# A kernel's build-time scheduler gets other durations for the instructions of each engine, and another delay between engines

## The chip, the cores and the metric

The kernel runs on one core of a Trainium2 chip. The metric is the device time of one execution, in microseconds (us), lower is better; a kernel's figure is the median of its runs. Engines are named as the profile names them: PE (TensorE), DVE (VectorE), ACT (ScalarE), POOL (GpSimd) and SP (SyncE, which issues DMA transfers).

## The reference, cut to what matters

One decoder block over 2048 positions with 1024 channels, in float32:

```
u    = rms_norm(x, norm1_gain);  proj = u @ w_in            # 1024 -> 3072
x_lru, g_lru, q, k, v, g_ret = split(proj)                  # six parts of 512
xc   = causal_conv4(x_lru);  hl = rg_lru(xc, gates)         # scan over positions
y_lru = rms_norm(hl * gelu(g_lru))
o    = head_group_norm(retention(rotary(q), rotary(k), v))  # 4 heads, chunks of 128
h    = x + concat(y_lru, o * silu(g_ret)) @ w_out           # 1024 -> 1024
u    = rms_norm(h, norm2_gain)
up   = causal_conv3(u @ ffn_up_w);  a, b = split(up)        # 1024 -> 6144
h    = h + (gelu(a) * b) @ ffn_down_w                       # 3072 -> 1024
return rms_norm(h, final_norm_gain)
```

## The kernel before, in words

**The matmuls.** A float32 product is made of three passes in a reduced float32 format: a high part times a high part, and each low part times the other's high part. The tiles are named for that: `wh` and `wl` (or `wv`) are the parts of the weights, `bh` and `raw` (`bl`) those of the activations. The high part is cut by ACT (`wh<-s`, `bh<-raw`), the low part by DVE (`wl<-s,wh`, `raw<-raw,bh`). Large matrix products are cut into units, and a unit into seven products instead of eight: sums of quadrants of the weights (`s`) and of the activations (named 11, T1, T2, 21, T3, T4, 22) are multiplied and combined again. One product is twelve matmuls of 128x512. The first four units (tile `pq`) and the output projection use the plain eight products. The banks in PSUM have the tags `x`, `y`, `e` and `sm` (1, 2, 2 and 3 of them): `px`, `py` and `pe` are the products of a unit, and `py` goes on accumulating after one partial result has been read out of it (that reading is called `u2` in the code).

**The stages.** Input projection (0 to about 320 us of the profile, its heads up to about 550), output projection (up to about 640), up-projection (640 to 1690), down projection (1690 to the end). Each is done in two halves of 1024 positions. Between the products of the projections stand small float32 matmuls: transposes of `o` (`pt<-idt,o`), the retention (`sc`, `pk`, `po`), the gates of the recurrence (`pa`, `pg`), sums for the norms (`mst`). A norm's factor goes one way through several engines: DVE (`ms`) to POOL (power of -0.5) to PE (transpose `pt<-idt,ms`) to ACT (`rb`) to SP (a row to memory and back, spread over the partitions).

**What sets the order.** The program is written as many generators (processes), one for each piece of work, each of which yields its operations in turn. A list scheduler (class `Flow`) runs them when the kernel is built, with a clock for each engine. In `run`, of all engines that one is taken whose next operation could start first; of its operations that are ready by then, the one of lowest rank (its priority, which comes from the tick at which it is due) is issued, and recorded as the next instruction of that engine. So the planned times decide one thing alone: the order of the instructions on each engine. On the chip each engine takes its instructions strictly in that order and waits for semaphores.

Four things enter the planned times. `Engine.cost_pe`, `cost_v`, `cost_a` and `cost_p` (from L129 on) give an operation's duration. `ready` gives the time at which its inputs are written and its output is free, and adds 0.2 us if the other engine is not the same. `issue` advances the engine's clock, adds 1.28 us when ACT has to load another table, and 0.1 us to the end of every operation of PE. The SP clock is held to the planned end of the transfers less `BACKLOG`. Slots of SBUF and banks of PSUM are handed out at planned times too (`grant`, `free`).

All instructions of the compute engines are recorded by one helper, so in the profile all of them stand on L127; DMA issues stand on L365 and, for the norms' rows, L1014.

Of the kernel before, what the change touches and what calls it, by code (L numbers as in the profile page):

```python
# [26 lines left out]
F32R = mybir.dt.float32r  # L27
AF = mybir.ActivationFunctionType
# [17 lines left out]
SMALL = 150  # L46
ORDER = ("l0 q0 v0 l1 q1 v1 l2 q2 v2 q3 v3 l3", "l3 q0 v0 l0 q1 v1 q2 v2 l1 q3 v3 l2")
RATE = 330.0
LATE = 16
PLAIN = 4  # L50
SOON = 2.5
# [26 lines left out]
ANY_TABLE = (AF.Copy, AF.Identity, AF.Square)  # L78
# [27 lines left out]
class Engine:  # L106
# [23 lines left out]

    def cost_pe(self, op, n, args, kw):
        if op == "transpose":
            return 0.13
        one = max(0.03, 0.0133 + n / 2400)
        if args[1].shape[0] == 64:
            one /= 2
        return one if args[1].dtype == F32R else 4 * one

    def cost_v(self, op, n, args, kw):
        if op == "tensor_tensor_scan":  # L140
            return 0.2 + 2.1e-3 * n
        if op in ("tensor_scalar", "tensor_copy", "memset"):
            return 0.15 + 0.535e-3 * n
        if op == "reciprocal":
            return 0.15 + 6.1e-3 * n
        if op == "bn_stats":
            return 0.3
        if op == "scalar_tensor_tensor":
            return 0.2 + 1.06e-3 * n
        return 0.15 + 1.05e-3 * n  # L150

    def cost_a(self, op, n, args, kw):
        us = 0.17 + 0.86e-3 * n
        if isinstance(kw.get("scale"), bass.AP):
            us += 0.1
        if isinstance(kw.get("bias"), bass.AP):
            us += 0.09
        if "accum_out" in kw:
            us += 0.2
        return us  # L160

    def cost_p(self, op, n, args, kw):
        return 0.1 if op == "dma_start" else max(1.0, 0.3 + 2.2e-3 * n)


class Event:
# [31 lines left out]
class Flow:  # L198
# [33 lines left out]
    def ready(self, op):  # L232
        t = 0.0
        for name in op.reads:
            w = self.wrote.get(name)
            if w:
                t = max(t, w[0] + (0.0 if w[1] == op.eng else 0.2))
        for name in op.writes:
            for table in (self.wrote, self.read):
                w = table.get(name)  # L240
                if w:
                    t = max(t, w[0] + (0.0 if w[1] == op.eng else 0.2))
        return t

    def issue(self, op, start):
        us = op.us
        if op.eng == "a" and op.func is not None and op.func not in ANY_TABLE and op.func not in self.table:
            self.table = next(t for t in TABLES if op.func in t)
            us += 1.28
        end = start + us  # L250
        self.clock[op.eng] = end
        if op.kb:
            end = self.dma = max(start + 1.7, self.dma) + op.kb / RATE
        if op.eng == "pe":
            end += 0.1
        for c in op.calls:
            c()
        for name in op.reads:
            if self.read.get(name, (0,))[0] < end:
                self.read[name] = (end, "dma" if op.kb else op.eng)  # L260
        for name in op.writes:
            self.wrote[name] = (end, "dma" if op.kb else op.eng)
# [65 lines left out]
def hymba_block_kernel(ctx: ExitStack, tc: tile.TileContext, xh, xn, win, wout, wup, down, gates, vecs,  # L328
# [1227 lines left out]
    def stage_b(g):  # L1556
        st = RawStage("B", g, m_d[g])
        ng = NormGroup(V_N2, u_d[g].put, h_d[g][0], LATE * g)
        us = []
# [160 lines left out]
```

## Time and profile before

| | |
|---|---|
| time, median of 3 runs | 2167.18 us |
| lowest, highest | 2165.2, 2167.5 us |
| span of the profiled execution | 2165.3 us (the execution's own time lies among the three above) |
| PE busy | 2143.6 us (99%), 9848 matmuls |
| DVE busy | 1729.8 us (80%), 2185 instructions |
| ACT busy | 1226.1 us (57%) |
| POOL busy | 38.3 us (2%) |
| DMA | 404.69 MB, 187 GB/s in the mean |

How to read it: a row of the timeline has its start and its duration in us, engine, line, operation, output and inputs, sizes, and how many are merged; in brackets stands the idle time before it and whom it waited for. A matmul's modelled duration (0.39 us) overlaps its neighbours', so a busy PE is not a measure of its speed; the distance from start to start is. In the view of waits, a row says who waited for whom: us in total, how many times, the longest.

### The profile page before, as it was taken

To read this page: it belongs to the slowest core of one execution; us is meant where nothing else is said; L and a number is where in the kernel's file an instruction comes from. 1 tells how busy PE (TensorE), PEld (TensorE's weight loads), DVE (VectorE), ACT (ScalarE), POOL (GpSimd) and SP (SyncE) were. 2 spreads that over 40 slices of the span, in tenths; PEclk is the share of its full clock that TensorE was granted. 3 is DMA by queue.
4 is the path that set the end of the run, shared out by engine and by line. 5 is a ranking of instruction groups with operands and counts; after the bars stand their busy time and mean duration, and the time that the engine had idled before them with its cause. 6 is when DMAs were issued, how large, how long until landed. Compare 5 with 4: busy or idle time off the path is not lost.

```text
span 2165.3 us, 26460 instructions
## 1 busy us (share of the span) xinstructions
PE 2143.6 (99%) x9848; PEld 1768.5 (82%) x9848; DVE 1729.8 (80%) x2185; ACT 1226.1 (57%) x1768; POOL 38.3 (2%) x32
## 2 busy tenths in 40 slices
PE   9999999999999999999999999999999999999998
PEld 7878887888878888888888888888888888888887
DVE  6999896877854789988878988787878977777776
ACT  6774668555652266666666866666666544334432
POOL 0000000000000000000000000000000000000000
PEclk9999999999999999999999999999999999999999
DMA  8966444431657935544233432322335777667674
GB/s 327 377 210 226 141 163 118 160 111 58 226 185 275 390 132 180 185 141 156 98 106 128 175 127 98 122 98 100 105 107 185 260 299 261 232 255 278 237 258 189
DMA packets 140768, 404.69 MB, mean 187 GB/s; under 512 B 15920, under 2 KB 20448, under 8 KB 140640
## 3 DMA queue, kind: packets, MB, share of 16 engines
q1 hardware_dynamic: 139344, 401.96, 52.7%
q8 instruction: 77, 1.26, 0.2%
q10 hardware_dynamic: 1296, 1.05, 0.1%
q14 instruction: 51, 0.42, 0.1%
HBM read 269.49 MB, written 125.07 MB: 182 GB/s over the span
## 4 chain that ended last, share of the span: by engine, by line
PE 92%; DVE 3%; DMA 3%; issue 1%; ACT 0%; SPq 0%; POOL 0%; DVEq 0%; ACTq 0%
PE py L127 33%; PE px L127 22%; PE pe L127 21%; PE pq L127 12%; PE po L127 1%; DMA raw<-in_dram 1%; PE pa L127 1%; PE pk L127 1%; PE sc L127 1%; PE pt L127 1%; DVE o L127 0%; PE mst L127 0%; DMA xt<-in_dram 0%; DMA x<-in_dram 0%; DVE wl L127 0%
## 5 line engine op out<-in xcount | busy, mean ns | idle before, releaser
L127 DVE TENSOR_TENSOR wl<-s,wh 128x1024 fp32r<-128x1024 f32 x172 | 210.2, 1222 | 113.4 <-ACT wh L127 108.7
L127 PE MATMUL px<-bh,wh 128*128 128x512 f32 x728 | 285.4, 392 | 1.4 <-DVE res L127 1.4
L127 PE MATMUL py<-bh,wh 128*128 128x512 f32 x728 | 285.9, 393 | 0.0
L127 PE MATMUL px<-raw,wh 128*128 128x512 f32 x728 | 283.8, 390 | 1.8 <-DVE raw L127 1.8
L127 PE MATMUL py<-bh,wl 128*128 128x512 f32 x728 | 283.9, 390 | 1.3 <-DVE wl L127 1.3
L127 PE MATMUL pe<-bh,wh 128*128 128x512 f32 x728 | 285.1, 392 | 0.0
L127 PE MATMUL pe<-raw,wh 128*128 128x512 f32 x728 | 283.7, 390 | 0.9 <-DVE raw L127 0.9
L127 PE MATMUL pe<-bh,wl 128*128 128x512 f32 x728 | 283.8, 390 | 0.7 <-DVE wl L127 0.7
L127 PE MATMUL py<-raw,wh 128*128 128x512 f32 x728 | 283.7, 390 | 0.0
L127 PE MATMUL px<-bh,wl 128*128 128x512 f32 x728 | 283.6, 390 | 0.0
L127 DVE SCALAR_TENSOR_TENSOR c<-o,vec,c 128x1022 f32<-128x1022 f32 x192 | 244.0, 1280 | 8.1 <-ACT c L127 3.3
L127 ACT CAST wh<-s 128x1024 fp32r<-128x1024 f32 x172 | 180.4, 1049 | 122.1 <-DVE s L127 107.1
L127 PE MATMUL py<-bh,wv 128*128 128x512 f32 x728 | 240.5, 391 | 1.9 <-DVE res L127 1.0
L127 ACT COPY o<-py 128x512 f32<-128x512 f32 x204 | 119.7, 587 | 167.1 <-PE py L127 163.5
L127 ACT CAST bh<-raw 128x1024 fp32r<-128x1024 f32 x158 | 162.2, 1050 | 68.0 <-DMA h<-res 27.4
L127 DVE TENSOR_TENSOR raw<-raw,bh 128x1024 fp32r<-128x1024 f32 x158 | 188.7, 1219 | 9.2 <-ACT bh L127 9.1
L127 PE MATMUL pq<-bh,wh 128*128 128x512 f32 (+1 forms) x432 | 168.0, 389 | 0.5 <-ACT bh L127 0.4
L127 PE MATMUL pq<-bh,wl 128*128 128x512 f32 (+1 forms) x432 | 165.2, 382 | 0.5 <-DVE wl L127 0.5
L127 PEld LDWEIGHTS py<-bh,wh 128*128 128x128 f32 x728 | 136.7, 188 | 33.1 <-issue 3.0
L127 PEld LDWEIGHTS py<-bh,wv 128*128 128x128 f32 x728 | 136.7, 188 | 32.7 <-ACT o L127 1.5
L127 PEld LDWEIGHTS px<-bh,wh 128*128 128x128 f32 x728 | 136.7, 188 | 31.3 <-DVE res L127 1.8
L127 PEld LDWEIGHTS py<-bh,wl 128*128 128x128 f32 x728 | 136.7, 188 | 30.8 <-DVE wl L127 2.1
(143 smaller groups left out, 3775.0 us busy)
## 6 DMA issues: line engine op xcount, KB each, us to landing
wa<-in_dram SPq DMA_DIRECT2D x86, 512.0 KB, 4.4
wb<-in_dram SPq DMA_DIRECT2D x86, 512.0 KB, 5.3
h<-res SPq DMA_DIRECT2D x56, 512.0 KB, 3.7
g_T<-t SPq DMA_DIRECT2D x96, 256.0 KB, 2.5
raw<-g_T SPq DMA_DIRECT2D x48, 512.0 KB, 5.7
res<-h SPq DMA_DIRECT2D x48, 512.0 KB, 7.2
g<-c SPq DMA_DIRECT2D x76, 256.0 KB, 4.2
raw<-g SPq DMA_DIRECT2D x38, 512.0 KB, 6.7
```

What stands on the lines that cost most here:

```text
L127: return Op(self.name, lambda: fn(*args, **kw), us, writes, reads, func=func)
```

## The change: other durations, and a delay for each engine that hands over

The diff replaces the numbers of the four cost functions, the 0.2 us of `ready` by a table with a delay for each producing engine, and takes away the 0.1 us that was added at the end of PE's operations. Nothing else is changed. A few of the durations that come out:

| operation | planned before | planned now |
|---|---|---|
| PE matmul 128x512, reduced format | 0.227 | 0.227 |
| PE transpose 128x128 | 0.13 | 0.11 |
| PE matmul 128x128, float32 | 0.267 | 0.267 |
| DVE tensor_tensor 1024 | 1.225 | 1.135 |
| DVE scalar_tensor_tensor 1024, pointer scalar | 1.285 | 1.195 |
| DVE tensor_tensor 512 | 0.688 | 0.601 |
| ACT copy 512 from PSUM | 0.610 | 0.486 |
| ACT cast 1024 from SBUF | 1.051 | 0.950 |
| POOL power 128x8 | 1.0 | 1.64 |

```diff
+LAG = {"pe": 0.21, "v": 0.13, "a": 0.15, "p": 0.13, "dma": 0.08}
...
     def cost_pe(self, op, n, args, kw):
         if op == "transpose":
-            return 0.13
-        one = max(0.03, 0.0133 + n / 2400)
-        if args[1].shape[0] == 64:
-            one /= 2
-        return one if args[1].dtype == F32R else 4 * one
+            return 0.11
+        if args[1].dtype == F32R:
+            return 0.0133 + n / 2400
+        one = max(0.111, 0.0266 + n / 1200)
+        return one * (1.23 if args[1].shape[0] == 64 else 2)
...
-            return 0.2 + 2.1e-3 * n
...
+            return 0.3 + 2.04e-3 * n
...
-        return 0.15 + 1.05e-3 * n
+        us = 0.068 + n / (1920 if op in ("tensor_scalar", "tensor_copy", "memset") else 960)
+        if any(isinstance(kw.get(k), bass.AP) for k in ("scalar", "scalar1")):
+            us += 0.06
+        return us
...
-        us = 0.17 + 0.86e-3 * n
...
+        us = 0.11 + (0.735e-3 if args[1].space == bass.MemoryType.PSUM else 0.82e-3) * n + 0.095 * aps
...
-        return 0.1 if op == "dma_start" else max(1.0, 0.3 + 2.2e-3 * n)
+        return 0.8 + 0.105 * n if n < 16 else 0.15 + 2.25e-3 * n
...
-                t = max(t, w[0] + (0.0 if w[1] == op.eng else 0.2))
+                t = max(t, w[0] + (0.0 if w[1] == op.eng else LAG[w[1]]))
...
-            us += 1.28
+            us += 1.295
...
-        if op.eng == "pe":
-            end += 0.1
```

What it does to the program: each engine keeps its set of instructions (PE 9848, DVE 2185, ACT 1722 beside the table loads, POOL 28, 973 transfers on SP), and the 769 products stay in the same order on PE. What is placed otherwise are the small groups between them, and the work of DVE, ACT and SP. Three pieces of the order follow.

On PE, near 107 us of the trace of before, the transpose of the norm's factor (`ms`, second half of the first norm) stood behind the second `po` group of the retention:

```order
L127 MATMUL po<-st,o_589 128x128
L127 MATMUL po<-vT,pm 128x128
L127 MATMUL pt<-idt,ms_271 8x128
L127 MATMUL pe<-bh,wh 128x512
L127 MATMUL pe<-raw,wh 128x512
L127 MATMUL pe<-bh,wl 128x512
```

Now, on PE too:

```order
L128 MATMUL pq<-bh,wl 128x512
L128 MATMUL pk<-vT,kT 128x128 x4
L128 MATMUL pt<-idt,ms_271 8x128
L128 MATMUL po<-st,o_575 128x128
L128 MATMUL po<-vT,pm 128x128
```

It has moved ahead of both `po` groups and of the product `px` between them.

On DVE, at the same place (104 to 122 us), the operation on `ms` that feeds POOL came ahead of the convolution of the recurrent branch (`xc`):

```order
L127 TENSOR_TENSOR raw<-raw,bh 128x1024 x2
L127 TENSOR_SCALAR ms_271<-ms_271 128x8
L127 TENSOR_TENSOR raw<-raw,bh 128x1024
L127 BN_STATS bn<-po 128x6 x4
L127 BN_AGGR ag<-bn 128x2 x4
L127 TENSOR_SCALAR rs<-ag,sml 128x4
L127 TENSOR_TENSOR raw<-raw,bh 128x1024
L127 TENSOR_TENSOR wl<-wa,wh 128x1024
L127 SCALAR_TENSOR_TENSOR rs<-ag,rs 128x4
L127 SCALAR_TENSOR_TENSOR xc<-o_985,vec,xc 128x1021
L127 SCALAR_TENSOR_TENSOR xc<-ctail,vec,xc 128x3
L127 SCALAR_TENSOR_TENSOR xc<-o_985,vec,xc 128x1022
```

Now, on DVE:

```order
L128 TENSOR_TENSOR o_1115<-pq,rb 128x512
L128 MEMSET st 128x128
L128 SCALAR_TENSOR_TENSOR xc<-o_977,vec,xc 128x1021
L128 SCALAR_TENSOR_TENSOR xc<-ctail,vec,xc 128x3
L128 SCALAR_TENSOR_TENSOR xc<-o_977,vec,xc 128x1022
L128 SCALAR_TENSOR_TENSOR xc<-ctail,vec,xc 128x2
L128 SCALAR_TENSOR_TENSOR xc<-o_977,vec,xc 128x1023
L128 SCALAR_TENSOR_TENSOR st<-st,pk 128x128 x4
L128 TENSOR_SCALAR ms_271<-ms_271 128x8
L128 SCALAR_TENSOR_TENSOR xc<-ctail,vec,xc 128x1
L128 COPY ctail<-o_977 128x3
L128 TENSOR_TENSOR raw<-raw,bh 128x1024
```

The convolution now comes first, and `ms` behind most of it.

On DVE near 362 to 380 us, the rotary operations on one `o` (three, with `rope` and `sw`) stood behind the scan of the recurrence (`xc<-ea,hlast,gi`):

```order
L127 TENSOR_TENSOR s_3318<-wb 128x512
L127 TENSOR_TENSOR s_3318<-wa,wb 128x512
L127 SCALAR_TENSOR_TENSOR tt<-ea,tt 128x1024
L127 TENSOR_TENSOR gi<-gi,tt 128x1024
L127 SCALAR_TENSOR_TENSOR xc<-ea,hlast,gi 128x1024
L127 COPY hlast<-xc 128x1
L127 TENSOR_TENSOR o_3314<-o_3314,pe 128x512
L127 TENSOR_TENSOR wl<-s_3122,wh 128x1024
L127 TENSOR_TENSOR xc<-xc,o_2920 128x1024
L127 TENSOR_TENSOR o_3072<-o_3072,rope 128x1024
L127 TENSOR_TENSOR sw<-sw,rope 128x1024
L127 TENSOR_TENSOR o_3072<-o_3072,sw 128x1024
```

Now, on DVE:

```order
L128 TENSOR_SCALAR ms<-mst 128x8
L128 TENSOR_TENSOR o_3069<-o_3069,rope 128x1024
L128 TENSOR_TENSOR sw<-sw,rope 128x1024
L128 TENSOR_TENSOR o_3069<-o_3069,sw 128x1024
L128 SCALAR_TENSOR_TENSOR tt<-ea,tt 128x1024
L128 TENSOR_TENSOR gi<-gi,tt 128x1024
L128 SCALAR_TENSOR_TENSOR xc<-ea,hlast,gi 128x1024
L128 COPY hlast<-xc 128x1
```

They have moved ahead of the operation `tt<-ea,tt`, which needs ACT's result, and the two sums `s` have moved back.

More of the change, by code (lines that the diff above doesn't have):

```diff
@@ L132, in cost_pe @@
         if op == "transpose":
-            return 0.13
-        one = max(0.03, 0.0133 + n / 2400)
-        if args[1].shape[0] == 64:
-            one /= 2
-        return one if args[1].dtype == F32R else 4 * one
+            return 0.11
[3 more added lines that the diff above has]
+        return one * (1.23 if args[1].shape[0] == 64 else 2)
     def cost_v(self, op, n, args, kw):
         if op == "tensor_tensor_scan":
-            return 0.2 + 2.1e-3 * n
-        if op in ("tensor_scalar", "tensor_copy", "memset"):
-            return 0.15 + 0.535e-3 * n
+            return 0.3 + 2.04e-3 * n
         if op == "reciprocal":
             return 0.15 + 6.1e-3 * n
[L146 to L149, printed above, removed]
-        return 0.15 + 1.05e-3 * n
+        us = 0.068 + n / (1920 if op in ("tensor_scalar", "tensor_copy", "memset") else 960)
+        if any(isinstance(kw.get(k), bass.AP) for k in ("scalar", "scalar1")):
+            us += 0.06
+        return us
     def cost_a(self, op, n, args, kw):
-        us = 0.17 + 0.86e-3 * n
-        if isinstance(kw.get("scale"), bass.AP):
+        aps = sum(isinstance(kw.get(k), bass.AP) for k in ("scale", "bias"))
+        us = 0.11 + (0.735e-3 if args[1].space == bass.MemoryType.PSUM else 0.82e-3) * n + 0.095 * aps
+        func = next((x for x in args if isinstance(x, AF)), None)
+        if aps and func is not None and func not in ANY_TABLE:
             us += 0.1
-        if isinstance(kw.get("bias"), bass.AP):
-            us += 0.09
         if "accum_out" in kw:
-            us += 0.2
+            us += 0.1
         return us
     def cost_p(self, op, n, args, kw):
-        return 0.1 if op == "dma_start" else max(1.0, 0.3 + 2.2e-3 * n)
+        return 0.8 + 0.105 * n if n < 16 else 0.15 + 2.25e-3 * n
 class Event:
@@ L241, in ready @@
                 if w:
-                    t = max(t, w[0] + (0.0 if w[1] == op.eng else 0.2))
+                    t = max(t, w[0] + (0.0 if w[1] == op.eng else LAG[w[1]]))
         return t
```

## The prediction

> **What bounds the kernel now.** I read the page first: the chain that ended last, by engine.
>
> ```profile
> PE 92%; DVE 3%; DMA 3%; issue 1%; ACT 0%; SPq 0%; POOL 0%; DVEq 0%; ACTq 0%
> ```
>
> TensorE (PE) holds 92% of the chain. A busy PE can still be a slow one, so next comes the chain in order of time, in an undisturbed part of the down projection: twelve matmuls (one product of a unit) follow the twelve before at 2.72 us, 0.227 us apart.
>
> ```profile
> 1848.78 2.72 PE px L127 x12
> 1851.50 2.72 PE py L127 x12
> ```
>
> The change neither removes nor shortens a matmul, and each engine's set of instructions stays what it was; so the time can move only where PE stands still. The view of waits, kept to PE and to the span from 20 us on, lists that idle time: us in total, times, longest.
>
> ```profile
> PE px L127 <- DVE raw L127: 1.8, 1, 1.8
> PE pb L127 <- POOL ms L127: 1.4, 2, 1.1
> PE px L127 <- DVE res L127: 1.4, 1, 1.4
> PE py L127 <- DVE wl L127: 1.3, 2, 1.0
> PE mst L127 <- DVE sqacc L127: 1.2, 1, 1.2
> PE py L127 <- DVE res L127: 1.0, 1, 1.0
> PE pt L127 <- DVE o L127: 0.9, 1, 0.9
> PE pe L127 <- DVE raw L127: 0.9, 1, 0.9
> PE py L127 <- ACT o L127: 0.8, 2, 0.4
> PE pe L127 <- DVE wl L127: 0.7, 1, 0.7
> ```
>
> These ten rows make 11.4 us, 0.5% of the span. What PE waits before 20 us hangs on the first loads, which the change leaves alone. So 11 us is about all that any new order can win, while what it can lose has no such end. What a measurement of this kernel tells from no change is about 0.2%, or 4.3 us.
>
> Where PE is short of work, VectorE (DVE) feeds it. The table by stretches (PE, PEld, DVE, ACT, POOL busy, then PE's granted clock, DMA share, GB/s) shows DVE nearly full in the input projection and with room in the up-projection:
>
> ```profile
> 100.00:200.00 100.00, 96.15 (x468) 78.03 (x467) 95.41 (x139) 64.36 (x84) 5.30 (x3) 1.00 0.69 239
> 642.00:1690.00 1048.00, 1048.00 (x4642) 868.21 (x4642) 855.55 (x947) 638.59 (x1017) 3.31 (x3) 1.00 0.44 156
> ```
>
> From 642 to 1690 us PE never stands still. New orders there swap work that already has cover, so I cost that half of the kernel at nothing; the cover is DVE's 192 idle us of 1048. If the cover were gone, what it costs is one evicting copy's delay, below 1 us a place.
>
> **The change part by part.** The new durations make DVE and ACT quicker and PE's small fp32 groups shorter in the plan. All 769 products keep their order on PE; what moves is the small groups between them (mostly by one or two products) and the work of DVE, ACT and SP.
>
> *First place, 104 to 125 us.* Here PE had its longest wait, 1.8 us at 122.67 for a `raw`. First PE, then DVE, then POOL:
>
> ```profile
> 107.03 0.39 PE L127 MATMUL po<-st,o 128*128 128x128 f32 x2
> ...
> 113.51 0.27 PE L127 MATMUL pt<-idt,ms 128*8 128x128 f32 x1
> ...
> 122.67 0.51 PE L127 MATMUL px<-raw,wh 128*128 128x512 f32 x1 [1.82 <-DVE raw L127]
> ```
>
> ```profile
> 106.50 0.69 DVE L127 TENSOR_TENSOR o<-pq,rb 128x512 f32<-128x512 f32 x1
> ...
> 110.67 0.16 DVE L127 TENSOR_SCALAR ms<-ms 128x8 f32<-128x8 f32 x1
> 110.74 1.22 DVE L127 TENSOR_TENSOR raw<-raw,bh 128x1024 fp32r<-128x1024 f32 x1
> ...
> 115.56 1.27 DVE L127 SCALAR_TENSOR_TENSOR xc<-o,vec,xc 128x1021 f32<-128x1021 f32 x1
> 116.76 0.21 DVE L127 SCALAR_TENSOR_TENSOR xc<-ctail,vec,xc 128x3 f32<-128x3 f32 x1
> ```
>
> ```profile
> 111.01 2.45 POOL L127 TENSOR_TENSOR ms<-ms,cst 128x8 f32<-128x8 f32 x1 [76.72 <-ACT bh L127]
> ...
> 687.87 1.63 POOL L127 TENSOR_TENSOR ms<-ms,cst 128x8 f32<-128x8 f32 x1 [45.83 <-DVE ms L127]
> ```
>
> Now the transpose `pt<-idt,ms` stands ahead of the `po` group, so PE comes to it at 107.0 less the 0.3 us won at the group of `pb` near 34 us (the `pb` row: 1.4 in two, the longer 1.1), at 106.7. On DVE, meanwhile, one `raw` (1.2 us) and most of the `xc` chain (three long ones at 1.2 from start to next start, two short at 0.2, 4.0 together) come ahead of `ms`; all that DVE had done by 106.5 is still ahead of it. Without any gain that puts `ms` at 106.5 + 5.2 = 111.7. There is a gain: before, DVE stood waiting for products of PE at six evictions between 54 and 101 us, and five of these now stand behind other work that is ready.
>
> ```profile
> DVE o L127 <- PE pq L127: 3.8, 6, 0.9
> ```
>
> I take 3.5 of the 3.8 us as won, since the sixth remains: `ms` at 108.2. From the start of `ms` on DVE to POOL's start go 0.34 us (110.67 to 111.01), from POOL's end to PE 0.05, and POOL takes 1.63 to 2.45, 2.0 in the middle. So `pt` starts near 110.6 and PE stands 3.9 us. With nothing won and the long POOL row it would be 7.8, with everything won and the short row 3.2. POOL, and PE's queue behind `pt` (the `po`, then `px`), all hang on it.
>
> The Trainium skill (GPSIMD Engine Reference, Specifications) says that GpSimd shares its SBUF interfaces with VectorE and contends with DVE instructions that have two SBUF inputs. This trace agrees so far as two rows can: 2.45 beside `raw` additions, 1.63 where DVE had nothing before it. By that rule the stall would be 0.4 more, since a `raw` addition stands right behind `ms` here too.
>
> What follows gains. The wait at 122.67 goes: PE comes to it 3.6 us later, and `raw` is ready no later than before. The waits on `wl` (0.7 near 156, 1.3 in two near 163 and 184) fall to DVE's finish, and DVE is ahead by up to 3.5 us while PE is behind: they go as well. In all: old waits of 0.3 + 1.8 + 2.0 = 4.1 against a new one of 3.9, a net of **-0.2**; between -0.9 and, with 7.8, +3.7.
>
> *Second place, 357 to 388 us.*
>
> ```profile
> 361.37 2.01 POOL L127 TENSOR_TENSOR ms<-ms,cst 128x8 f32<-128x8 f32 x1 [36.37 <-DVE ms L127]
> ```
>
> ```profile
> 366.78 1.23 DVE L127 SCALAR_TENSOR_TENSOR tt<-ea,tt 128x1024 f32<-128x1024 f32 x1 [3.04 <-ACT tt L127]
> ```
>
> ```profile
> 363.81 0.27 PE L127 MATMUL pt<-idt,ms 128*8 128x128 f32 x1
> ...
> 387.53 0.63 PE L127 MATMUL pt<-idt,o 128*128 128x128 f32 x4 [0.93 <-DVE o L127]
> ```
>
> DVE waits 3.04 us for ACT here. The three rotary operations on `o` (1.2 each), which stood behind `xc`, now stand ahead of that wait and fill it, and SP issues the table's second load (`rope`) ahead of the row that it must wait for. What is left of DVE's work until 387 us is shorter by those three, so the 0.9 at 387.53 goes: **-0.9** (0 if the chain only gets stuck elsewhere). The price: the `pt<-idt,ms` at 363.81 moves one product (2.72 us) earlier and had only 0.43 us to spare behind POOL (361.37 + 2.01 = 363.38).
>
> *Small groups one product earlier.* Two more are like it (the transposes of `o` near 179 us and a `po` near 414 us). Each costs nothing when its producer moved as far, and 2.72 at most. Of the 92 places where such groups stand, four waited before, for 0.3 to 1.2 us; I take 0.6 each, three times, **+1.8** (0 to 8.2).
>
> *Down projection, 1690 to the end.* One gain, three losses of one kind:
>
> ```profile
> 1693.59 0.69 DVE L127 TENSOR_TENSOR res<-res,py 128x512 f32<-128x512 f32 x1 [1.31 <-PE py L127]
> ...
> 1849.17 0.68 DVE L127 TENSOR_TENSOR res<-res,py 128x512 f32<-128x512 f32 x1
> ```
>
> At 1693.59 DVE idled 1.31 us for a product; the addition goes behind two ready operations, so the next operands come some 1.3 earlier and the 0.9 of `pe` for `raw` goes: **-0.9**. At 1849.17 the addition that reads the accumulating `py` goes behind a `wl` and a `raw`, 1.2 each: it ends at 1849.17 + 2.4 + 0.68 = 1852.2, where PE adds into the same `py` from 1851.5 on, as the chain above has it. That is a stall of 0.7 if DVE runs as before, and none if it is 0.7 early; I take 0.4. The same stands 152 us later, and near 2100 us a scaling of `h` goes ahead of such an addition: **+1.2** (0 to 2.1). At the very end the `mst` group stands behind the last product and two scalings ahead of it: **+0.4** (0 to the 1.2 of its row now).
>
> The waits for `res` (1.4 and 1.0) keep their order and stay. For the two on ACT's `o` (0.8) some of ACT's work moves ahead and some behind: nothing.
>
> **The sum.** -0.2 - 0.9 + 1.8 - 0.9 + 1.2 + 0.4 = +1.4 us. It is made against the profiled execution, whose span of 2165.3 is 0.1 above the lowest of the three times (2165.2) and 1.9 under their median (2167.2). Carried to the median: **2168.6**.
>
> **The rivals.**
>
> *Faster: DVE's recovered idle removes most waits.* For it: waits on DVE make 9.2 of the 11.4 us, and early evictions that stalled DVE are just what truer PE lengths mend. If the new wait at `pt` is also short (1 us), the terms are 4.1 - 1 won at the first place, 0.9 + 0.9, the 0.8 for ACT and the small groups free, with half of the losses (0.8): -4.9, 2162.3. With the `res` waits too, -7.3. Against it: the wait on POOL starts from a DVE that is 95% busy.
>
> *Slower: small groups block PE.* One mechanism: PE takes matmuls strictly in order, and a small group set ahead of its producer stops the products behind it. Place: `pt<-idt,ms` at 107 us, then those at 179, 364 and 414. Price: +3.7 at the first (nothing recovered) and three times 1.4 (half a product), and the sum's other terms (-0.9 - 0.9 + 1.2 + 0.4) of -0.2: +7.7, 2174.9. It decides when `ms` on DVE starts after 110 us. Against it: the plan only put `pt` there because it reckons its producer done.
>
> *The clock falls in a long stall.* The longest idle time of PE in mid-kernel was 1.8 us, and the clock stayed whole; over the tail, where PE goes idle for good, it is 0.81 (the row from 100 to 200 us above has 1.00).
>
> ```profile
> 2150.00:2165.30 15.30, 5.80 (x47) 5.36 (x45) 10.83 (x26) 2.00 (x5) 2.92 (x4) 0.81 0.74 263
> ```
>
> If a 3.9 us stall does the same, the loss is between 0 and 0.19 x 15.3 = 2.9 us, at the most 2171.5. The Trainium skill (TensorE: Matmul & The Clock Gate, What's actually happening) puts the gate's window near 3.4 us of idling, after which the array runs at half speed until a window has been busy; by it my estimate is 1.7 us, and it speaks against a change that trades several short waits for one long one. No mid-kernel stall in this trace is long enough to test it.
>
> *The order does not matter.* Gains and losses may be hidden under neighbours alike: 2167.2.
>
> **How the numbers follow.** The forecast, 2168.6 (its own range 2164 to 2172), 0.40; faster 0.25; slower 0.20; the clock 0.05; no effect 0.10. Leaving out a tenth at each side, the range goes from 2162 (the faster case's value) to 2174.5 (just under the slower one's). Faster by over 0.2%: 0.25. Slower: 0.20, and 0.05 from the forecast's upper edge, 0.25. Within: the rest, 0.50.
>
> **What would show it.** In the profile after, the waits of PE should show `pt <- POOL ms` of 3 to 4 us near 107, no `px <- DVE raw` of 1.8, no `wl` rows near 156 and 163, and no `pt <- DVE o` near 387; the `pe <- DVE raw` gone, new `py <- DVE res` of 0.4 at three places; DVE's waits for `pq` before 101 us under 1 us. A granted clock under 1.00 between 107 and 116 would be the gate. A wait of PE in 642 to 1690 us, or one over 2 us that stands nowhere here, makes the reasoning wrong even if the time fits; a total of PE's waits that moved by over 4 us makes the forecast wrong.

## The result, and the profile after

The changed kernel takes **2190.14 us** (median; 2188.65 to 2192.9), the kernel before in the same session 2166.97 us (2165.2 to 2167.5). The ratio is 1.011, 95% interval 1.0096 to 1.0125: slower by 23 us. The prediction was 2168.6 with a range up to 2174.5; it was wrong.

The profiled execution has a span of 2188.8 us against 2165.3, so 23.5 us are to be found. The page's chain has PE at 86% where it was 92%, with DVE, DMA and ACT taking the rest:

```profile
span 2188.8 us, 26534 instructions
...
PE 86%; DVE 6%; DMA 4%; ACT 2%; issue 1%; SPq 0%; POOL 0%; DVEq 0%; ACTq 0%; POOLq 0%
```

The waits of PE from 20 us on, after (before, ten rows made 11.4 us):

```profile
PE pe L128 <- DVE o L128: 5.6, 2, 3.5
PE px L128 <- ACT o L128: 3.7, 2, 2.1
PE py L128 <- ACT o L128: 2.9, 2, 1.7
PE pt L128 <- POOL ms L128: 2.8, 1, 2.8
PE pb L128 <- POOL ms L128: 2.3, 2, 1.2
PE py L128 <- ACT y L128: 2.2, 2, 1.8
PE py L128 <- DVE res L128: 2.2, 3, 0.9
PE py L128 <- DVE wl L128: 1.9, 1, 1.9
PE py L128 <- ACT py L128: 0.8, 1, 0.8
PE sc L128 <- ACT vT L128: 0.6, 1, 0.6
PE pt L128 <- DVE pm L128: 0.5, 1, 0.5
PE pq L128 <- DVE o L128: 0.5, 1, 0.5
PE pa L128 <- PE px L128: 0.2, 1, 0.2
```

They make 26.2 us, 14.8 more. Two of the top three rows are new in kind: `o` on ACT is the copy, and on DVE the addition (`o<-o,pe`), that empties a bank of PSUM, and PE waits for it because its next product goes into that bank. All of them but `pb` and `res` lie before 640 us; from 640 to 1690 us PE stands still nowhere, as before.

Most of the other 8.7 us are no waits at all. Four times PE runs on at a lower granted clock after a wait. The table by stretches (PE, PEld, DVE, ACT, POOL busy, then the granted clock) around the waits at 165.44 and 584.89 us:

```profile
165.00:170.00 5.00, 4.56 (x13) 3.65 (x14) 3.53 (x5) 0.84 (x2) 0.00 (x0) 0.66 0.97 288
```

```profile
585.00:590.00 5.00, 5.00 (x15) 3.95 (x16) 4.83 (x5) 4.05 (x5) 0.00 (x0) 0.66 0.82 222
```

And the matmuls in the second of them, from start to start 0.23 us, then 0.43 for some 3 us, then 0.24 again:

```profile
584.89 0.50 PE L128 MATMUL pe<-bh,wh 128*128 128x512 f32 x1 [3.51 <-DVE o L128]
585.23 0.40 PE L128 MATMUL pe<-raw,wh 128*128 128x512 f32 x1
585.47 0.52 PE L128 MATMUL pe<-bh,wl 128*128 128x512 f32 x1
585.79 0.63 PE L128 MATMUL pe<-bh,wh 128*128 128x512 f32 x1
586.21 0.63 PE L128 MATMUL pe<-raw,wh 128*128 128x512 f32 x1
586.64 0.63 PE L128 MATMUL pe<-bh,wl 128*128 128x512 f32 x1
```

Clock 0.66 over 5 us is 1.7 us lost (0.34 x 5). The other two such places, after the waits at 247.65 and 293.51, come to 1.7 as well, so 6.8 us in all. 14.8 + 6.8 = 21.6 of the 23.5 us; the remaining 1.9 are not placed.

How one such wait comes about, at 247.65 us. ACT (start, duration, idle time before in brackets):

```profile
241.45 0.58 ACT L128 COPY o<-py 128x512 f32<-128x512 f32 x1
246.06 1.06 ACT L128 ACTIVATE sqt<-xc 128x1024 f32<-128x1024 f32 x1 [4.03 <-DVE xc L128]
247.03 0.57 ACT L128 COPY o<-px 128x512 f32<-128x512 f32 x1
```

The copy `o<-px` is short, but stands behind a square that waits 4 us for DVE; DVE's `xc` there is late because its own chain waited for ACT:

```profile
239.64 1.23 DVE L128 SCALAR_TENSOR_TENSOR tt<-ea,tt 128x1024 f32<-128x1024 f32 x1 [5.28 <-ACT tt L128]
```

PE waits 2.07 us for the copy. In the stretch from 100 to 640 us the two engines that feed PE wait for one another more. DVE, before and then after:

```profile
DVE sw L127 <- DMA rope<-in_dram: 7.5, 3, 4.2
DVE wl L127 <- ACT wh L127: 7.2, 7, 2.1
```

```profile
DVE wl L128 <- ACT wh L128: 25.6, 17, 6.5
DVE o L128 <- DMA rope<-in_dram: 15.1, 6, 5.0
...
DVE rs L128 <- POOL rs L128: 7.7, 8, 1.2
```

ACT, before and then after:

```profile
ACT o L127 <- PE py L127: 53.7, 37, 5.2
...
ACT wh L127 <- DVE s L127: 13.8, 12, 2.6
...
ACT y L127 <- DVE rs L127: 6.5, 5, 4.3
```

```profile
ACT y L128 <- DVE rs L128: 39.4, 12, 12.6
ACT o L128 <- PE py L128: 37.6, 21, 4.3
ACT wh L128 <- DVE s L128: 32.3, 18, 4.9
```

Summed over all rows of that stretch, ACT waited 133.7 us for PE and 54.7 for DVE before; after, 98.4 for PE and 104.1 for DVE. DVE waited 55.8 us for PE and 23.7 for ACT before; after, 37.0 for PE and 48.7 for ACT. An engine that waits for PE's products has time in hand over PE; these sums say that DVE and ACT have less of it now. They do not set the loss by themselves: `table_only` below loses 13 us with sums near those of before (58.1 for ACT on DVE, 22.0 for DVE on ACT), and `costs_alone` loses 10 with 77.6 and 43.1.

### The profile page after: what moved, and what is told of

Read it like the earlier page. It is cut to its first block, busy times and chain, and to the rows that moved or that the text cites. A ratio compares the mean times of both kernels' runs of the same rounds, so it can differ in the third digit from the quotient of the medians.

```text
span 2188.8 us, 26534 instructions
## 1 busy us (share of the span) xinstructions
PE 2152.8 (98%) x9848; PEld 1773.6 (81%) x9848; DVE 1731.4 (79%) x2185; ACT 1218.9 (56%) x1768; POOL 42.1 (2%) x32
## 4 chain that ended last, share of the span: by engine, by line
PE 86%; DVE 6%; DMA 4%; ACT 2%; issue 1%; SPq 0%; POOL 0%; DVEq 0%; ACTq 0%; POOLq 0%
PE py L128 31%; PE pe L128 21%; PE px L128 20%; PE pq L128 11%; DMA wa<-in_dram 1%; DVE wl L128 1%; PE po L128 1%; DVE xc L128 1%; DVE res L128 1%; DVE raw L128 1%; DVE o L128 1%; DMA sw<-o 1%; PE pa L128 1%; DVE s L128 1%; PE pk L128 1%
## 5 line engine op out<-in xcount | busy, mean ns | idle before, releaser
L128 DVE SCALAR_TENSOR_TENSOR c<-o,vec,c 128x1022 f32<-128x1022 f32 x192 | 245.8, 1281 | 24.0 <-ACT c L128 18.3
L128 ACT ACTIVATE c<-o,vec 128x1024 f32<-128x1024 f32 x96 | 119.5, 1245 | 87.2 <-DVE o L128 86.3
L128 PEld LDWEIGHTS pe<-bh,wh 128*128 128x128 f32 x728 | 137.0, 188 | 36.6 <-DVE o L128 6.5
```

Source lines behind the costliest of these rows:

```text
L128: return Op(self.name, lambda: fn(*args, **kw), us, writes, reads, func=func)
```

## The experiments

Five theories stand in the expectations. A: the old durations were too long and so held a margin, which the new ones take away. B: the order of before is one good one among many, and any departure costs. C: what is missing in the plan is the time of transfers. D: each wait is one engine's queue, and a local swap mends it. E: the feeders are late as a whole, and a swap only changes who is waited for. The numbers below are medians in us and ratios to the kernel before, each with its 95% interval; the waits of PE (from 20 us on) and the clock's loss (summed over stretches of 5 us with a clock under 0.995, the last 25 us left out) are those of the run's profile.

**1. One part of the change alone.** The delays alone, `lag_alone`:

```diff
+LAG = {"pe": 0.21, "v": 0.13, "a": 0.15, "p": 0.13, "dma": 0.08}
-                t = max(t, w[0] + (0.0 if w[1] == op.eng else 0.2))
+                t = max(t, w[0] + (0.0 if w[1] == op.eng else LAG[w[1]]))
-        if op.eng == "pe":
-            end += 0.1
```

> Before with the new delays between engines and without the 0.1 us at the end of PE's operations; all durations as before. Theory A (lost margin: the old durations were too long, so the chip ran ahead of the plan and covered what the plan leaves out, transfers above all; the new ones leave nothing): the durations still carry the margin, so little is lost, 0 to +8 us against before, PE's waits from 20 us on 10 to 18 us. Theory B (any shuffle costs: the order of before is one good one among many, and the direction of the change matters little): +8 to +25 us.

DVE's durations alone (`v_alone`: the new `cost_v` and nothing else of the diff):

> Before with the new durations of DVE alone. Theory A: DVE is the fullest of the feeding engines, so its margin is the largest part: +6 to +16 us, with new waits of PE on DVE or on ACT behind DVE. Theory B: +5 to +25 us, waits anywhere.

ACT's durations alone (`a_alone`: the new `cost_a`, and 1.295 for the table load):

> Before with the new durations of ACT alone (table load included). Theory A: a smaller part than DVE's, +3 to +10 us, the waits being PE on ACT. Theory B: +5 to +25 us, waits anywhere.

And the smallest part there is, `table_only`:

```diff
-            us += 1.28
+            us += 1.295
```

> Before with the table load at 1.295 instead of 1.28 us and nothing else: 15 ns for some 30 loads, no margin lost. Theory A: within 3 us of before. Theory B: the order shuffles all the same, +5 to +20 us.

| | us | ratio | PE's waits | clock's loss |
|---|---|---|---|---|
| before | 2166.39 | 1 | 11.4 | 0 |
| lag_alone | 2185.59 | 1.009 (1.007 to 1.011) | 24.1 | 5.2 |
| v_alone | 2197.12 | 1.0145 (1.0123 to 1.0166) | 30.5 | 15.3 |
| a_alone | 2175.37 | 1.0042 (1.0026 to 1.0058) | 15.7 | 1.7 |
| table_only | 2179.84 | 1.0066 (1.0046 to 1.0085) | 19.8 | 3.4 |

Three parts alone cost 59 us together (19 + 31 + 9) where the whole costs 23: the parts do not add up, each is another order (PE's and POOL's durations alone were not run). And 15 ns on the table load, of which the profile of before has 39, cost 13 us. Theory A had put that within 3 us and `lag_alone` at 8 at most: in its simple form it is wrong. `v_alone` lies above the ranges of both theories. What 15 ns did, in PE's waits from 100 to 640 us:

```profile
PE py L127 <- ACT o L127: 5.3, 4, 2.9
PE py L127 <- DVE wl L127: 5.2, 1, 5.2
PE px L127 <- DVE raw L127: 1.8, 1, 1.8
```

The third row is before's own; the first two are ten us of waits of the kinds that the whole change brings.

**2. A margin given back, transfers made longer.** `after_lagpad`: the changed kernel with

```diff
-LAG = {"pe": 0.21, "v": 0.13, "a": 0.15, "p": 0.13, "dma": 0.08}
+LAG = {"pe": 0.41, "v": 0.33, "a": 0.35, "p": 0.33, "dma": 0.28}
```

> The changed kernel with 0.2 us more on each of the five delays (the new durations kept): a margin for every hand-over. Theory A (lost margin): most of the loss comes back, 2168 to 2177 us, and the chip runs level with the plan or ahead of it. Theory B (any shuffle costs; a 15 ns edit of the order's numbers has already cost 13 us): another random order, 2175 to 2200 us, no better than the changed kernel on the whole.

`after_dma` is the changed kernel, `before_dma` the one before, with

```diff
-            end = self.dma = max(start + 1.7, self.dma) + op.kb / RATE
+            end = self.dma = max(start + 3.7, self.dma) + op.kb / RATE
```

> The changed kernel with a transfer's planned landing 2 us later (3.7 us instead of 1.7 before its bytes), nearer to the 4.4 to 8.8 us that the traces show for 512 KB against the planned 3.3. Theory C (what stalls the changed kernel is waits of DVE and ACT on transfers that the plan has too short, with PE's feeders queued behind them): those waits shrink and the time falls by 8 us or more, to 2182 or under. Theory A without C: no more than 5 us won. Theory B: a random order, 2175 to 2200.

> The kernel before with the same later landing of transfers. Theory C: the waits on transfers matter here too, so 0 to 6 us faster than before. Theory A: margin added, no loss: within 4 us of before. Theory B: the order of before is a picked one, so any other costs, +8 to +25 us.

`after_table`: the changed kernel with 1.28 in place of 1.295:

> The changed kernel with the table load back at 1.28 us: 15 ns, about 110 rows of difference on DVE. Theory A: within 3 us of the changed kernel. Theory B: wherever the order differs the time may move by several us either way, 2180 to 2198.

| | us | ratio | PE's waits | clock's loss |
|---|---|---|---|---|
| after_lagpad | 2180.82 | 1.0068 (1.0045 to 1.0091) | 21.3 | 3.4 |
| after_dma | 2185.75 | 1.0089 (1.0066 to 1.0112) | 22.2 | 8.5 |
| before_dma | 2182.72 | 1.0081 (1.0057 to 1.0105) | 21.9 | 8.5 |
| after_table | 2188.33 | 1.0101 (1.0078 to 1.0124) | 25.3 | 5.2 |

Theory C falls: with longer transfers in the plan the changed kernel won 4 us, not 8, and before lost 16. That loss is a miss of A as well, which had put `before_dma`, a plan with more margin, within 4 us of before; it is what B had put. The margin on the delays won 9 us: less than A had put (2168 to 2177), and inside B's range, though B had expected it no better than the changed kernel. `after_table` differs from the changed kernel in few places and is level with it, as A had it, and B's range holds it as well.

**3. Swaps by hand.** `after_held` records eleven operations behind the one that PE was seen to wait for, and leaves the rest of the order; `before_held` does so at four places of before. The edit is a list (engine, index of the operation: index of the one behind which it is recorded) and a few lines in `issue`:

```diff
+HOLD = {('a', 167): 168, ('a', 243): 244, ('a', 388): 389, ('a', 275): 276, ('v', 466): 468, ('v', 467): 468,
+        ('v', 564): 566, ('v', 565): 566, ('v', 135): 137, ('v', 136): 137, ('v', 192): 193}
...
-        for c in op.calls:
-            c()
+        k = self.count[op.eng] = self.count.get(op.eng, -1) + 1
+        if (op.eng, k) in HOLD:
+            self.held.setdefault((op.eng, HOLD[op.eng, k]), []).extend(op.calls)
+        else:
+            for c in op.calls + self.held.pop((op.eng, k), []):
+                c()
```

> The changed kernel with eight local swaps and nothing planned anew: eleven operations of DVE and ACT are recorded behind the one that PE waits for (the scan behind the eviction of pe near 460 and 585 us, sqrt and square roots of ACT behind the eviction of px or py near 247, 357 and 575, a cast behind px near 398, a scaling behind wl near 165, the convolution and the state behind ms near 108). Theory D (each stall of PE is one engine's queue: what PE needs is ready and stands behind an operation that waits or is long): the eight waits of 1.2 to 3.5 us fall by 14 us together, and with them two or more of the four falls of the clock at 1.7 us each, so 2168 to 2176 us. Rival E (the feeders are late as a whole, the swap only changes who is waited for): less than 6 us won, 2184 or more.

> The kernel before with four such swaps: part of the convolution behind raw near 122 us, a scaling behind wl near 163, two convolution steps behind raw near 1709, a raw and a wl behind the addition that frees px near 1739. Theory D: PE's waits there fall from 5.6 to about 1.5 us, 2161 to 2164.5 us, faster than both kernels by a little more than the measurement tells. Rival E: within 1 us of before, the waits come back one operation later.

| | us | ratio | PE's waits | clock's loss |
|---|---|---|---|---|
| after_held | 2189.50 | 1.0105 (1.009 to 1.0121) | 24.8 | 6.8 |
| before_held | 2166.50 | 0.9997 (0.9988 to 1.0006) | 10.6 | 0 |

Theory D falls, E stands. In `after_held` the eight waits fell from 16.9 us to 4.5 (five are gone; 1.5 is left near 109, 0.7 near 165 and 2.3 near 585). The wait for `o<-px` at 247 us is one of those that are gone, since the copy now runs 3.8 us earlier. ACT in `after_held`:

```profile
243.26 0.59 ACT L129 COPY o<-px 128x512 f32<-128x512 f32 x1 [0.72 <-PE px L129]
246.58 1.06 ACT L129 ACTIVATE sqt<-xc 128x1024 f32<-128x1024 f32 x1 [2.73 <-DVE xc L129]
```

But ten us later PE waits 3.0 us for DVE instead, and the same happens elsewhere (at 181, 411, 476 and 486 us). PE's waits in `after_held`, the first five rows:

```profile
PE pt L129 <- DVE o L129: 5.7, 2, 3.0
PE pt L129 <- POOL ms L129: 2.6, 2, 1.5
PE pe L129 <- DVE o L129: 2.3, 1, 2.3
PE pb L129 <- POOL ms L129: 2.3, 2, 1.2
PE sc L129 <- ACT vT L129: 2.1, 1, 2.1
```

So 12.4 us went at the eight places and 11.0 came elsewhere: 1.4 won in all (26.2 to 24.8), and the clock falls at four places, as in the changed kernel. In `before_held` the two waits at 1709 and 1739 us went, the one at 122 fell from 1.8 to 1.3, the one at 163 stayed at 1.0, and one of 1.0 came at 1717; 0.8 us won in all, which the times do not show.

**4. All durations, old delays; and a nudge that does next to nothing.** `costs_alone` is the changed kernel's four cost functions and table load with the 0.2 and the 0.1 of before. `rate_331` is the kernel before with `RATE = 331.0` for 330.

> All new durations with the delays of before (0.2 us from any other engine, 0.1 us at PE's end). Theory A (lost margin): part of the margin is there, 2172 to 2184 us, faster than the changed kernel. Theory B (any shuffle costs): one more random order, 2175 to 2200 us, on either side of the changed kernel's.

> The kernel before with the planned transfer rate at 331 instead of 330 (0.3%, under 5 ns for 512 KB) and no duration or delay changed. Theory B: about 400 rows of the order differ on PE, DVE and ACT, so some loss, 2168 to 2180 us. Theory A: no loss, within 2 us of before.

`costs_alone` takes 2176.47 us, 1.0046 (1.0031 to 1.0061): 14 us faster than the changed kernel, with the same durations, and inside the ranges of both theories. `rate_331` takes 2165.49, 0.9998 (0.9988 to 1.0007), level with before though some 400 rows stand otherwise: so not every departure costs, which is against B as it was put.

**5. Luck or level.** One kernel of a kind cannot tell whether a plan is worse or only unluckier. So two nudges (small edits of a number that should not matter) without any margin in them were put on three plans each (before; new durations with old delays; the changed kernel): `RATE = 300.0` (`_rate`), and `c[0] <= t + 0.08` for `0.05` in `run`, the limit up to which an operation counts as ready (`_tol`).

> The kernel before with the planned transfer rate at 300 instead of 330. Theory A (a margin in the plan is worth 10 us or more on the average, each order having luck of some us beside it): 2166 to 2178 us. Theory B (the order of before is a picked one, any other is as good or bad as the changed kernel's): 2175 to 2195.

> New durations, old delays, planned rate 300. Theory A: 2172 to 2184 us, by some 10 us under the changed kernel with the same nudge. Theory B: 2175 to 2195, no order between the three.

> The changed kernel with the planned rate 300. Theory A: 2183 to 2197 us, the slowest of the three. Theory B: 2175 to 2195, no order between the three.

> The kernel before where an operation counts as ready within 0.08 us instead of 0.05. Theory A (a margin is worth 10 us or more on the average): 2166 to 2178 us. Theory B (any order but the picked one is as good or bad as the changed kernel's): 2175 to 2195.

> New durations, old delays, readiness within 0.08 us. Theory A: 2172 to 2184 us. Theory B: 2175 to 2195, no order between the three.

> The changed kernel, readiness within 0.08 us. Theory A: 2183 to 2197 us, the slowest of the three. Theory B: 2175 to 2195, no order between the three.

| plan | as it is | rate 300 | ready within 0.08 | other nudges |
|---|---|---|---|---|
| before | 2166.4 | 2172.15, 1.0024 (1.0013 to 1.0036) | 2174.7, 1.0044 (1.0029 to 1.006) | 2165.5, 2179.8, 2182.7 |
| new durations, old delays | 2176.5 | 2196.74, 1.0138 (1.0108 to 1.0167) | 2175.21, 1.0039 (1.0019 to 1.0059) | |
| changed kernel | 2190.1 | 2192.67, 1.0119 (1.009 to 1.0149) | 2190.79, 1.0114 (1.0085 to 1.0143) | 2188.3, 2185.75 |

The five nudged versions of before have a mean of 2175.0; the changed kernel's four have 2189.4. No nudged version of before is as slow as any of the changed kernel's. In these means the loss has two parts: before's own order lies about 9 us under its neighbours' mean, and the changed plan's neighbours lie some 14 us above before's. (`before_dma` and `after_dma`, among the others, move the plan by 2 us for each transfer and are no small nudges; without them the means are 2173.0 and 2190.6.) B's "no order between the three" is wrong for the first and the last; A's mean is right for these two, but the plan in the middle scatters over 21 us (2175.2 to 2196.7) and does not tell how much of the 14 us goes to the durations and how much to the delays. `costs_rate`, 2196.7, lies above the ranges of both theories, and `before_rate` and `before_tol` lie under B's. A nudged version shares most of its order with the plan it comes from, so five of a kind are not five independent draws; how firm the 14 us are stays open, and so does whether they come from lost margin or from something else in the new plan, such as the slots and banks that are handed out at planned times: no run separates these.

**The account.** Over all twenty profiles (before, after and these eighteen), the span less 2165.3 is the added waits of PE plus the clock's loss to within 3.1 us: `v_alone` 33.2 against 19.1 + 15.3, `costs_rate` 30.4 against 18.3 + 13.6, `table_only` 12.2 against 8.4 + 3.4, `a_alone` 6.3 against 4.3 + 1.7. So where the time goes is shown; why the new plan brings more waits is shown only as far as the means above go.

No version here beats the kernel before by more than the measurement tells.

## Why the prediction was wrong, point by point

**What bounds the kernel: right, and its ceiling too.** PE's standing time is what moved, with its clock behind it, and no order among these won more than 2 us. By the prediction's own signs its reasoning failed, and not the number alone: it had named as such a sign a wait over 2 us that stands nowhere in it, and there are three on evictions (3.5, 2.1 and 2.1 us); and PE's waits moved by 14.8 us, where it had allowed 4.

**The half from 642 to 1690 us: right for this order.** It was costed at nothing and PE waits nowhere in it. But the cover is not sure, and the price put on its loss (below 1 us a place) is too low: in `before_rate`, `after_rate`, `costs_rate`, `before_dma` and `after_dma` PE waits 2.8 or 2.9 us for `wh` near 740 to 765 us, and its clock falls behind that wait.

**First place: right in kind, then it failed.** `pt<-idt,ms` did wait for POOL's `ms`, 2.8 us against 3.9; the wait for `raw` went (1.8), as did those at 156 and 184. But "DVE is ahead by up to 3.5 us while PE is behind: they go as well" failed at 165.44, where `wl` came 1.9 us late, and the clock fell behind it. DVE in fact started `ms` at 107.71, within 0.5 us of the 108.2 worked out, and it waited for no `pq` before 101 us, so its gain up to there was real; but from 108 to 165 us it waited 7.7 us for ACT and transfers (4.1 of them for ACT's `tt`), where before it had waited 2.9.

**POOL beside DVE.** In the after trace `ms` takes 1.64 us beside a `raw` addition, just what it takes with DVE idle, but that addition begins 0.14 us behind it:

```profile
108.02 1.64 POOL L128 TENSOR_TENSOR ms<-ms,cst 128x8 f32<-128x8 f32 x1 [73.61 <-DVE xc L128]
```

```profile
108.16 1.21 DVE L128 TENSOR_TENSOR raw<-raw,bh 128x1024 fp32r<-128x1024 f32 x1
```

Before, the addition had begun 0.27 us ahead of POOL (110.74 against 111.01), and POOL took 2.45. The twenty profiles hold 140 such powers of 128x8 and agree without exception. The 55 that start while DVE runs an operation with two inputs in SBUF take 1.92 to 3.75 us; the other 85, with DVE idle or reading PSUM at their start, take 1.63 or 1.64, whatever DVE begins beside them. So the rule of the Trainium skill (GPSIMD Engine Reference, Specifications) is borne out. The prediction's reading of the queue was wrong: two short operations stand between `ms` and the addition, POOL starts ahead of it, and the 0.4 did not come.

**Second place: right on the step, wrong beside it.** The wait of `pt` at 387 is gone and the one at 363 did not come. New ones stand beside them: 1.2 us at 357.76 and 1.6 at 398.40, both for ACT's copies.

**Small groups one product early: wrong.** None of the three named groups waits. The small groups that do wait (`py<-idt,y` 1.8 at 293.51, `sc` 0.6, `pt` for `pm` 0.5) were not named.

**Down projection: near.** The wait for `raw` at 1709 is gone, two new waits for `res` stand (0.6 at 1873.44, the first place named, and 0.7 at 2070.33, which was not named, against 0.4 each for three), and the wait of 1.4 that was to stay went too. The end did not get longer: its two waits for POOL and DVE made 2.3 (1.1 and 1.2) and make 2.3 now.

**The step that failed.** It is the sentence "For the two on ACT's `o` (0.8) some of ACT's work moves ahead and some behind: nothing." ACT's evictions cost 6.6 us now (3.7 + 2.9), from 0.8, and those on DVE, for which the sum has no term at all, 5.6: emptying the banks takes 12.2 us. The sum went through the places where PE waited before and where PE's own rows had moved; it did not go through the feeders' queues, where a copy that frees a bank had come to stand behind an operation that waits for another feeder. The `Slower` rival looked at PE's queue for that as well. The experiments by hand show that even a full list of such places would not have given the number: a swap moves the wait on to the next place.

**The clock: right that it can fall, wrong in place and size.** The rival had a chance of 0.05 and at most 2.9 us, at 107 to 116 us. There the granted clock stayed at 1.00; it fell at four other places and took 6.8 us. The estimate by the Trainium skill (TensorE: Matmul & The Clock Gate, What's actually happening), 1.7 us for one fall, is what each of the four falls measures. Its condition is met by one of the four alone: the page puts the gate at an idle window near 3.4 us, and the wait at 584.89 was 3.5 us, but waits of 1.8, 1.9 and 2.1 us brought a fall about as well, while one of 2.78 (at 109.72) did not, nor one of 2.1 (at 460.47), nor before's 1.8. The measurement decides: a wait of some 2 us may cost nearly as much again.

**The range.** With terms that were each of the right kind the sum gave +1.4, and the spread was taken from those terms. What a new order can do was never priced as such: 15 ns on one number of the plan moved the time by 13 us, more than the whole range on that side.

## What to carry to other kernels

When a change only reorders work in front of a full engine, the price of the change is not the sum over the places that waited before: look at the feeders, and at what they wait for. If they wait for the full engine, they have time in hand; where an edit makes them wait for one another, a delay in the chain can reach the full engine, and here swaps at the places where it showed mostly passed it on. A greedy order that was measured and kept is a picked one: nudge a number that should not matter before reading a gain or a loss into one that should, and compare means over nudges.

## What the runs showed of the hardware that was not expected

A PE that stood still for about 2 us may run its next 3 us at half its rate (after the wait of 1.87 us at 165.44 as after that of 3.51): 0.43 us from matmul to matmul against 0.23, and 1.7 us lost. A longer wait can cost twice that: in `before_tol`, 3.5 us behind the one of 4.1 at 370.74. The losses of all runs are multiples of 1.7 (1.7, 3.4, 5.2, 6.8, 8.5, 13.6, 15.3, to 0.1). In the twenty profiles, from 20 to 2120 us, a lower clock (the mean over the next 5 us) followed each of the 30 waits of 2.80 us or more, and 13 of the 46 from 1.60 up to that; in that band the length of a wait did not tell which.

A power of 128x8 on POOL is longer (1.92 to 3.75 us against 1.64) when DVE is already running an operation with two inputs in SBUF at its start; one that DVE begins later does not lengthen it.
